# Feed-forward blocks taken in pairs with one down phase, the layer-2 start without norm edges, and a wider bonus product, in a two-layer RWKV-7 / S5 trunk

## The chip, the cores and the metric

The kernel runs on one core of a Trainium2 chip. The metric is the device time in microseconds of one execution, from the first to the last instruction. The engines named below are PE (TensorE, matrix products), PEld (its load of the stationary operand), DVE (VectorE), ACT (ScalarE), POOL (GpSimd) and SP (SyncE, which issues most DMAs).

## The reference

A sequence of 1024 frames of 1024 features passes two layers. Layer 0 mixes the frames by RWKV-7 (16 heads of 64), layer 1 by a diagonal complex state-space layer (S5) with a gated output; each mixer is followed by a squared-ReLU feed-forward part of width 4096, and every sub-layer ends in a layer norm of `alpha * h + f(h)`.

```python
def sq_relu_mlp(x, w1, w2):
    return jnp.square(jax.nn.relu(x @ w1)) @ w2
...
    bonus = jnp.sum(rh * kh * r_k.astype(f32), axis=-1, keepdims=True) * vh
    o = o + bonus.reshape(bsz, seq, d)
    return (o.astype(x.dtype) * g) @ wo
...
    for i in range(DEPTH):
        ...
        h = layer_norm(DN_ALPHA * h + mix, ln_g[2 * i], ln_b[2 * i])
        h = layer_norm(DN_ALPHA * h + sq_relu_mlp(h, mlp_w1[i], mlp_w2[i]),
                       ln_g[2 * i + 1], ln_b[2 * i + 1])
```

## The kernel before

**Tiles.** Features lie on the 128 partitions, frames on the free axis. The 1024 frames are two halves of 512 columns, A (tiles `hA`, operands `oAh`/`oAl`) and B (`hB`, `oBh`/`oBl`); a half of the residual is 8 tiles of 128x512.

**Dense products.** Each operand is split into a rounded high part and the rest. `mm3` (L258, through `mmb`, so that most rows have L256) computes one 128x128 by 128x512 product as three matmuls: high weight by high data, high weight by low data, low weight by high data. A weight comes by DMA into `wraw` (SP), ACT casts it to `whi` (L191), DVE takes the rest into `wlo` (L192); four buffers of each.

**Feed-forward part.** The width of 4096 is 16 blocks of 256 (`KB2` = 2 tiles). `up(b)` computes two 128x512 tiles, 24 matmuls each, and turns each into a pair of operands: ACT takes relu (L1126) and square (L1127) and casts the high part into `qbuf` (L191), DVE takes the low part (L192). This is called the power chain here. `down(b)` runs over the 8 output tiles: each gets 6 matmuls (2 tiles by 3) into a PSUM tile `d`, and DVE adds that to the residual tile `hA` or `hB` (L1158; L1156, which also scales, for the first block). `mlp` runs up(0), then for each block up(b+1), down(b), and yields once a block, so that between an up and its own down phase lie the 48 matmuls of the next up.

**Bonus.** In `elem` of the RWKV part, each of 16 calls computes the bonus sums of two heads in eight chunks of 64 frames: 16 products of a 64x64 piece of `kf` by a column of `rksel` into `pb` (L648), then one DVE copy to `bo` (L650).

**Order.** The program is written step by step, but a scheduler with a timeline model orders every engine's queue by the rank of each step and by its estimate of when the operands are there. A few edges are fixed by hand: `weave` puts steps of a second generator (a norm, splits of weights) behind chosen DVE adds, `inorder` and `behind` fix neighbours. INS1 and INS3 say after how many turns of a feed-forward part the next part's code is emitted; PACEU, PACED and PREB set how much is woven in.

**PSUM.** The products `d` of the RWKV and layer-1 feed-forward parts take turns in three banks. One bank, tag "l", is shared by the triangular inverse of the RWKV units (`pv`, and the lines from L716 on, 30 steps on DVE one after the other, L716 and L718) and by the layer norm's sums (`pm` L989, `pq` L934, `pr` L957). Two banks are for "a" and two for "c". From the layer-2 feed-forward part on, `d` has seven.

**Stages in time** (us from the start of the profiled execution): loads and the RWKV projections to 120; the RWKV units of both halves with the projections and the output product `wo` (its adds are L1110) to about 770, in which the norm of A (LN1: means `pm`, centring L993, variance `pq`, L939 to L942 the result and its split) stands at 681 to 714; feed-forward of A with `wo` of B; from 1010 the S5 tables beside it; S5 of A (1300 to 1410); feed-forward of B with S5 of B at 1665 to 1790; the gates; from 1904 layer 2's feed-forward part, where three blocks (`JB`) of A are done alone with the norm of B woven into the adds of `da(0)` and `da(1)`, thirteen blocks are done for both halves together by `both`, and three of B at the end. The last two of these run in column halves of 256, with the last norm (`last_norm`, L1036 to L1088) of the first half under the products of the second.

Of the kernel before, what the change touches and what calls it, by code (L numbers as in the profile page):

```python
# [18 lines left out]
HT = 512  # L19
KT = 8  # L20
L = 64
KB2 = 2
INS1 = 12
INS2 = 13
VSH = (-1, 2, 2, 4, 64)
INS3 = 12
# [6 lines left out]
TB = 2  # L33
# [3 lines left out]
PACEU = (2.0, 7.0)  # L37
PACED = (0.5, 1.3)
PREB = 3
JB = 3  # L40
# [39 lines left out]
def trunk(ctx, tc, A):  # L80
# [123 lines left out]
    nw = [0]  # L204
# [373 lines left out]
    def elem(m):  # L578
# [5 lines left out]
        for j in range(2):  # L584
# [60 lines left out]
            for c in range(8):  # L645
                for h in range(2):
                    hs, bs = slice(64 * h, 64 * h + 64), slice(64 * (1 - h), 64 * (1 - h) + 64)
                    PE.matmul(pb[bs, c : c + 1], kf[hs, c * L : (c + 1) * L], rksel[hs, n0 + c // 4, h : h + 1],  # L648
                              start=True, stop=True)
            V.tensor_copy(ci(D.bo), pb[:, 0:8].rearrange("p (i c) -> p i c", i=2))  # L650
# [463 lines left out]
    def blocks(i, h, xo, qbuf):  # L1114
# [27 lines left out]
        def down(b, first=False, cs=slice(0, HT), keep=None):  # L1142
            for n2 in range(C // nw):
                if keep is None:
                    w = wload(A["mw2"][i, b, n2], KB2, nw, ("mw2", i, b, n2))
                else:
                    if (b, n2) not in keep:
                        keep[b, n2] = kept(A["mw2"][i, b, n2], low[("mw2", i, b, n2), 0])
                    w = keep[b, n2]
                for n in range(nw // 128):  # L1150
                    p = psd()[:, cs]
                    dense(p, [(x[:, n * 128 : (n + 1) * 128], y[:, n * 128 : (n + 1) * 128]) for x, y in w],
                          [(x[:, cs], y[:, cs]) for x, y in qs[b]])
                    z = h[n2 * (nw // 128) + n][:, cs]
# [7 lines left out]
    def mlp(i, h, xo, qbuf):  # L1162

        nb = 32 // KB2
        up, down = blocks(i, h, xo, qbuf)
        up(0)
        for b in range(nb):
            if b + 1 < nb:
                up(b + 1)
            down(b, b == 0)  # L1170
            yield
# [484 lines left out]
    first_steps(second_half(), 99000)  # L1656
    for b in range(JB - 1):
        ua(b + 1)
        da(b, b == 0)
    unweave()  # L1660
# [11 lines left out]
    da(JB - 1, JB == 1)  # L1672
# [12 lines left out]
    for b in range(JB - TB):  # L1685
        ub(b + 1)
        db(b)
    for b in range(JB - TB + 1, JB):
        ub(b)
    keep = {}  # L1690
    for c in range(2):
        for b in range(JB - TB, JB):
            db(b, False, slice(256 * c, 256 * c + 256), keep)
# [78 lines left out]
```

## Time and profile before

| | |
|---|---|
| median of 3 runs | 2558.89 us (2570.18, 2558.74, 2558.89) |
| profiled execution | 2565.43 us |
| its span | 2563.6 us |
| mean granted TensorE clock | 0.973 of full speed |
| PE busy | 2470.6 us in 16684 records |
| DVE busy | 1784.2 us in 3443 |
| ACT busy | 1213.8 us in 2165 |
| POOL busy | 409.6 us in 336 |
| DMA | 340.66 MB, mean 133 GB/s |

Busy time is the time in which an engine has an instruction under way. PE is busy 96% of the span, but its matmuls overlap, and a busy PE is not yet PE at its peak; what remains to be gained or lost by a new order is in the stretches where it stands still, 93 us in all, and in the stretches where the granted clock is under 1. So the profile is read stage by stage, by the idle time of PE in each, and then by what ended that idle time.

### The profile page before, as it was taken

The numbers are of one execution on the slowest core, as the hardware profiler recorded it, in microseconds if no ns is written. First come the engines' busy times: TensorE is split into PE (matmuls) and PEld (weight loads), VectorE is DVE, ScalarE is ACT, GpSimd is POOL, SyncE is SP. The second block draws the span as 40 slices with busy tenths as digits, with TensorE's granted clock in tenths as the row PEclk, the third lists the DMA queues.
The fourth block names the chain that finished last, engine by engine and source line by source line (L and its number), as shares of the span: only waits on it lengthen the run. The fifth ranks groups of instructions, "written<-read, shape, count | busy, mean of one in ns | idle before, by whom it ended". The sixth has DMA issues, their size and how long they took to land.

```text
span 2563.6 us, 43894 instructions
## 1 busy us (share of the span) xinstructions
PE 2470.6 (96%) x16684; PEld 2012.9 (79%) x16684; DVE 1784.2 (70%) x3443; ACT 1213.8 (47%) x2165; POOL 409.6 (16%) x336
## 2 busy tenths in 40 slices
PE   7999999999889999999998999999999999999997
PEld 5778777788768877877787788887887888888887
DVE  7478686687696867989876665676748555555556
ACT  7556665555354444345543444343555333333434
POOL 3111333232212011001000000100223111111101
PEclk9999998989899999999999999999999999999999
DMA  5875555654222335246556553244351111111233
GB/s 167 279 229 194 185 169 164 215 176 134 77 63 85 97 92 168 92 120 174 151 198 238 173 180 108 95 158 164 103 190 62 46 54 54 50 54 47 82 116 115
DMA packets 217682, 340.66 MB, mean 133 GB/s; under 512 B 21248, under 2 KB 81792, under 8 KB 217472
## 3 DMA queue, kind: packets, MB, share of 16 engines
q1 hardware_dynamic: 216320, 335.77, 41.3%
q8 instruction: 131, 2.15, 0.4%
q10 hardware_dynamic: 1152, 2.10, 0.2%
q14 instruction: 79, 0.65, 0.1%
HBM read 267.53 MB, written 70.25 MB: 132 GB/s over the span
## 4 chain that ended last, share of the span: by engine, by line
PE 79%; DVE 10%; DMA 5%; ACT 4%; issue 2%; POOL 0%; SPq 0%; ACTq 0%; DVEq 0%; POOLq 0%
PE d L256 59%; PE d L1195 9%; PE pA L672 1%; PE pR L780 1%; DVE wlo L192 1%; DVE oAl L192 1%; PE pX L785 1%; PE pk L1427 1%; DVE xh L718 1%; DVE x L716 1%; PE pU L790 1%; PE pq L934 1%; PE pb L648 1%; PE pO L801 1%; PE pO L799 1%
## 5 line engine op out<-in xcount | busy, mean ns | idle before, releaser
L191 ACT CAST whi<-wraw 128x512 fp32r<-128x512 f32 x424 | 262.2, 620 | 431.9 <-PE d L256 351.3
L192 DVE TENSOR_TENSOR wlo<-wraw,whi 128x512 fp32r<-128x512 f32 x424 | 308.6, 730 | 198.6 <-ACT whi L191 187.4
L256 PE MATMUL d<-qbuf,whi 128*128 128x512 f32 x1152 | 366.4, 399 | 9.5 <-ACT rl L1126 5.7
L256 PE MATMUL d<-oAh,whi 128*128 128x512 f32 (+1 forms) x752 | 303.5, 409 | 10.5 <-ACT ev L493 4.9
L256 PE MATMUL d<-oAl,whi 128*128 128x512 f32 (+1 forms) x752 | 300.8, 402 | 6.5 <-DVE oAl L942 4.4
L256 PE MATMUL d<-oAh,wlo 128*128 128x512 f32 (+1 forms) x752 | 301.7, 403 | 0.0
L256 PEld LDWEIGHTS d<-qbuf,whi 128*128 128x128 f32 x1152 | 213.7, 190 | 60.4 <-ACT rl L1126 7.4
L256 PE MATMUL d<-qbuf,wlo 128*128 128x512 f32 x576 | 227.7, 396 | 0.0
L256 PE MATMUL d<-oBh,whi 128*128 128x512 f32 x496 | 196.5, 397 | 0.0
L256 PE MATMUL d<-oBh,wlo 128*128 128x512 f32 x496 | 195.1, 394 | 0.0
L256 PE MATMUL d<-oBl,whi 128*128 128x512 f32 x496 | 194.8, 393 | 0.0
L256 PEld LDWEIGHTS d<-oAh,whi 128*128 128x128 f32 (+1 forms) x752 | 143.5, 192 | 45.3 <-ACT ev L493 6.3
L256 PEld LDWEIGHTS d<-oAl,whi 128*128 128x128 f32 (+1 forms) x752 | 143.7, 192 | 37.5 <-DVE oAl L942 4.8
L256 PEld LDWEIGHTS d<-oAh,wlo 128*128 128x128 f32 (+1 forms) x752 | 143.8, 192 | 30.9 <-issue 1.0
L256 PE MATMUL d<-qh,wlo 128*128 128x512 f32 x416 | 163.1, 392 | 0.0
L256 PE MATMUL d<-qh,whi 128*128 128x512 f32 x416 | 162.5, 394 | 0.0
L256 PE MATMUL d<-ql,whi 128*128 128x512 f32 x416 | 161.9, 389 | 0.0
L256 PEld LDWEIGHTS d<-qbuf,wlo 128*128 128x128 f32 x576 | 109.2, 190 | 23.5
L1158 DVE TENSOR_TENSOR hB<-hB,d 128x512 f32<-128x512 f32 (+1 forms) x160 | 98.0, 630 | 26.3 <-PE d L256 25.3
L256 PEld LDWEIGHTS d<-oBh,wlo 128*128 128x128 f32 x496 | 93.4, 188 | 21.2 <-issue 0.6
L1158 DVE TENSOR_TENSOR hA<-hA,d 128x512 f32<-128x512 f32 x136 | 91.9, 681 | 26.1 <-PE d L256 25.1
L256 PEld LDWEIGHTS d<-oBh,whi 128*128 128x128 f32 x496 | 93.6, 189 | 20.8 <-issue 0.9
(495 smaller groups left out, 5292.3 us busy)
## 6 DMA issues: line engine op xcount, KB each, us to landing
wraw<-in_mw_dram SPq DMA_DIRECT2D x356, 256.0 KB, 2.8
wlo<-low SPq DMA_DIRECT2D x92, 256.0 KB, 3.0
wraw<-in_glu_dram SPq DMA_DIRECT2D x64, 256.0 KB, 2.7
low<-wlo SPq DMA_DIRECT2D x52, 256.0 KB, 3.3
raw<-in_mw_dram SPq DMA_DIRECT2D x52, 256.0 KB, 2.6
wraw<-in_wk_dram SPq DMA_DIRECT2D x32, 256.0 KB, 3.5
wraw<-in_wr_dram SPq DMA_DIRECT2D x32, 256.0 KB, 4.4
wraw<-in_wv_dram SPq DMA_DIRECT2D x32, 256.0 KB, 4.9
```

Of the source, the lines that this page charges most:

```text
L191: S.copy(hi, src)
L192: op = (e or V).tensor_sub(lo, src, hi.bitcast(F32))
L256: bulk.append((PE.matmul(p, w, x, **kw).ins, x.shape[-1]))
L648: PE.matmul(pb[bs, c : c + 1], kf[hs, c * L : (c + 1) * L], rksel[hs, n0 + c // 4, h : h + 1], start=True, stop=True)
L672: prods.append(PE.matmul(pp[h][:, cc, i], D.KB[j][hs, u].rearrange("p j l -> p (j l)"), D.AR[j][hs, u].rearrange("p j l -> p (j l)"), star ...
L716: V.tensor_mul(tv, xa[:, s + 1 : 32, s : s + 1].broadcast_to([128, nt, w]), xv[:, s : s + 1, 0:w].broadcast_to([128, nt, w]))
L718: V.tensor_add(xv[:, s + 1 : 32, 0:w], xv[:, s + 1 : 32, 0:w], tv)
L780: hop.append(PE.matmul(pR[hs, i], at[:, h, c, i, 0], vsa[:, cl, h, i], start=True, stop=True))
L785: hop.append(PE.matmul(pX[hs, i], xt[hs, NP * c + i], R[hs, i], start=True, stop=True))
L790: hop.append(PE.matmul(pU[hs, i], D.kbt[i // 2, c // 2][:, c % 2, i % 2, hs], vsa[:, cl, h, i], start=True, stop=True))
L1158: weave(V.tensor_add(z, z, p), PACED[i])
L1195: PE.matmul(p, w[:, k], x, start=not add and k + j == 0, stop=k == 3 and j == 2, skip_group_check=True)
```

## The change

There are four edits.

1. `down` takes a tuple of blocks. Its two PSUM tiles for a pair of output tiles are summed over all blocks of the tuple, so that DVE adds once an output tile instead of once a block and output tile. For the first pair of output tiles the last block's two parts come last, one by one. `mlp` runs up(b), up(b+1), down((b, b+1)): 8 turns instead of 16, with INS1 and INS3 at 6 instead of 12, and other paces.
2. At the start of layer 2 the norm of B is emitted in one piece under rank 99000, without the edges of `weave`, ahead of up(1); da((0, 1)) follows, then up(2), the sums for `both`, and da((2,)).
3. In the last stage the first of B's three blocks has its down phase after up(1), and the last two share one down phase in each column half.
4. The bonus sums of both heads and two chunks of 64 frames come from one product of 128x128 by 2 columns: 4 products a call instead of 16. Four small copies (two on DVE, two on ACT) take the place of one.

```diff
-INS1 = 12
+INS1 = 6
...
-INS3 = 12
+INS3 = 6
...
-PACEU = (2.0, 7.0)
-PACED = (0.5, 1.3)
-PREB = 3
+PACEU = (2.0, 6.0)
+PACED = (0.5, 2.0)
+PREB = 1
...
-            for c in range(8):
-                for h in range(2):
-                    hs, bs = slice(64 * h, 64 * h + 64), slice(64 * (1 - h), 64 * (1 - h) + 64)
-                    PE.matmul(pb[bs, c : c + 1], kf[hs, c * L : (c + 1) * L], rksel[hs, n0 + c // 4, h : h + 1],
-                              start=True, stop=True)
-            V.tensor_copy(ci(D.bo), pb[:, 0:8].rearrange("p (i c) -> p i c", i=2))
+            for tt in range(4):
+                PE.matmul(pb[:, 2 * tt : 2 * tt + 2], kf[:, tt * 128 : (tt + 1) * 128], rksel[:, n0 + tt // 2],
+                          start=True, stop=True)
+            pbv = pb[:, 0:8].rearrange("p (i c h) -> p c i h", i=2, c=2)
+            for h in range(2):
+                for e in range(2):
+                    (V.tensor_copy if e == 1 - h else S.copy)(
+                        D.bo[64 * (1 - h) : 64 * (1 - h) + 64, e::2, 2 * j : 2 * j + 2],
+                        pbv[64 * e : 64 * e + 64, :, :, h])
...
-        def down(b, first=False, cs=slice(0, HT), keep=None):
+        def down(bs, first=False, cs=slice(0, HT), keep=None):
             for n2 in range(C // nw):
...
-                for n in range(nw // 128):
-                    p = psd()[:, cs]
-                    dense(p, [(x[:, n * 128 : (n + 1) * 128], y[:, n * 128 : (n + 1) * 128]) for x, y in w],
-                          [(x[:, cs], y[:, cs]) for x, y in qs[b]])
-                    z = h[n2 * (nw // 128) + n][:, cs]
+                nn = nw // 128
+                ps = [psd()[:, cs] for _ in range(nn)]
+                parts = [(w[k], qs[b][k]) for w, b in zip(ws, bs) for k in range(KB2)]
+
+                def products(n, js):
+                    for j in js:
+                        (x, y), (qh, ql) = parts[j]
+                        sl = slice(n * 128, (n + 1) * 128)
+                        mm3(ps[n], x[:, sl], y[:, sl], qh[:, cs], ql[:, cs], j == 0, j == len(parts) - 1)
+
+                last = len(parts) - 1
+                groups = [range(KB2 * m, KB2 * m + KB2) for m in range(len(bs))]
+                if n2 == 0 and len(bs) > 1:
+                    groups[-1:] = [(j,) for j in groups[-1]]
+                turns_ = [(n, js) for js in groups for n in range(nn)]
+                for n, js in turns_:
+                    products(n, js)
+                    if last not in js:
+                        continue
+                    z, p = h[n2 * nn + n][:, cs], ps[n]
...
-        up(0)
-        for b in range(nb):
-            if b + 1 < nb:
-                up(b + 1)
-            down(b, b == 0)
+        for b in range(0, 32 // KB2, 2):
+            up(b)
+            up(b + 1)
+            down((b, b + 1), b == 0)
             yield
...
     ua(0)
-    first_steps(second_half(), 99000)
-    for b in range(JB - 1):
-        ua(b + 1)
-        da(b, b == 0)
-    unweave()
+    with rank(99000):
+        run(second_half())
+    ua(1)
+    da((0, 1), True)
+    ua(2)
...
-    da(JB - 1, JB == 1)
+    da((2,))
...
-    for b in range(JB - TB):
-        ub(b + 1)
-        db(b)
-    for b in range(JB - TB + 1, JB):
-        ub(b)
+    ub(1)
+    db((0,))
+    ub(2)
     keep = {}
     for c in range(2):
-        for b in range(JB - TB, JB):
-            db(b, False, slice(256 * c, 256 * c + 256), keep)
+        db(tuple(range(JB - TB, JB)), False, slice(256 * c, 256 * c + 256), keep)
```

**What stands where.** The edits also move instructions that they do not touch, since the scheduler orders everything anew. Three places show it; after the change most lines have a number that is 3 higher up to about L1140 and about 20 higher behind it.

The first is PE where the output product of half A (`d<-oA`, weights `whi` and `wlo`) runs out and LN1's mean `pm<-hA` comes. Before, `pm<-hA` follows a few rows behind the last dense product:

```order
L256 MATMUL d<-oAh,wlo 128x512
L256 MATMUL d<-oAh,whi 128x512
L648 MATMUL pb<-rksel,kf 64x1 x3
L672 MATMUL pA<-AR,KB 128x128
L648 MATMUL pb<-rksel,kf 64x1 x13
L256 MATMUL d<-oAl,whi 128x512
L256 MATMUL d<-oAh,wlo 128x512
L790 MATMUL pU<-vsa,kbt 64x64 x8
L799 MATMUL pO<-st,AR 64x64 x8
L801 MATMUL pO<-vsa,AT_7131 64x64 x8
L672 MATMUL pA<-AR,KB 128x128 x2
L989 MATMUL pm<-hA,ones_c 128x512
```

After, the same engine goes from the last dense product into a run of small products of the RWKV units:

```order
L256 MATMUL d<-oAl,whi 128x512
L256 MATMUL d<-oAh,wlo 128x512
L793 MATMUL pU<-vsa,kbt 64x64 x8
L802 MATMUL pO<-st,AR 64x64 x8
L804 MATMUL pO<-vsa,AT 64x64 x8
L611 MATMUL pss<-hsel,sq 128x2 x4
L783 MATMUL pR<-vsa,AT 64x64 x8
L788 MATMUL pX<-o,XT 64x64 x8
L619 MATMUL pn<-ident,sq 128x128 x4
```

and comes to the mean 24 rows behind that last dense product, at the end of this piece:

```order
L740 MATMUL pv_7294<-XT,x_7220 32x32 x32
L619 MATMUL pn<-ident,sq 128x128 x4
L646 MATMUL pb<-rksel,kf 128x2 x4
L788 MATMUL pX<-o,XT 64x64
L992 MATMUL pm<-sa,ones_c 128x512
L992 MATMUL pm<-sb,ones_c 128x512
L992 MATMUL pm<-hA,ones_c 128x512
```

So the dense products of `wo` no longer lie among the last unit's small products.

The second place is DVE there: the adds of `wo` (L1110 before, L1113 after) against the steps of the fifth unit's inverse (`x` and `xh`, L716 and L718 before, L719 and L721 after). Before, six of the eight adds come behind the inverse's step of 128x117; the last of them stands 7 rows ahead of LN1's centring (L993):

```order
L650 COPY bo<-pb 128x2x4
L1110 SCALAR_TENSOR_TENSOR hA<-hA,d 128x512
L844 SCALAR_TENSOR_TENSOR o<-o,vr,lg 128x64
L793 TENSOR_TENSOR st<-pU,st 128x256
L844 SCALAR_TENSOR_TENSOR o<-o,vr,lg 128x64 x7
L192 TENSOR_TENSOR wlo<-wraw,whi 128x512
L794 TENSOR_TENSOR st<-st,PL 128x256
L622 SCALAR_TENSOR_TENSOR ldsg<-cmask,ldsg 128x512
L993 TENSOR_TENSOR hA<-hA,pm 128x512 x8
```

After, the eighth add stands right ahead of that step, 67 rows ahead of the centring (L996), and one split of a weight (L192) follows it:

```order
L847 SCALAR_TENSOR_TENSOR o<-o,vr,lg 128x64 x6
L789 COPY vsa<-pX 64x256
L721 TENSOR_TENSOR xh<-xh,x_7220 128x14x9
L1113 SCALAR_TENSOR_TENSOR hA<-hA,d 128x512
L719 TENSOR_TENSOR x_7220<-xa,xh 128x117
L192 TENSOR_TENSOR wlo<-wraw,whi 128x512
L721 TENSOR_TENSOR xh<-xh,x_7220 128x13x9
L796 TENSOR_TENSOR st<-pU,st 128x256
L719 TENSOR_TENSOR x_7220<-xa,xh 128x120
```

So the inverse and the following unit's element work now lie wholly between the last add and the norm.

The third place is PE in a feed-forward part of layer 1, half B, at the start of a down phase (numbers tell the buffers apart; `d_16877` and `d_16878` are the first pair of output tiles, `d_16917` the next; `whi_16867` belongs to the pair's first block, `whi_16873` and `whi_16913` to blocks of the second). After the change it reads, from the last product of the up phase:

```order
L256 MATMUL d_16823<-oBh_12255,wlo_16833 128x512
L256 MATMUL d_16877<-qbuf_9489,whi_16867 128x512 x2
L256 MATMUL d_16877<-qbuf_9489,wlo_16868 128x512
L256 MATMUL d_16877<-qbuf_9489,whi_16867 128x512 x2
L256 MATMUL d_16877<-qbuf_9489,wlo_16868 128x512
L256 MATMUL d_16878<-qbuf_9489,whi_16867 128x512 x2
L256 MATMUL d_16878<-qbuf_9489,wlo_16868 128x512
```

and the products that use the second tile of the up phase just ended come here, first by the high part of `q` (single rows), then by the low and the high:

```order
L256 MATMUL d_16917<-qbuf_9489,whi_16913 128x512 x2
L256 MATMUL d_16917<-qbuf_9489,wlo_16914 128x512
L256 MATMUL d_16877<-qbuf_9489,whi_16873 128x512
L256 MATMUL d_16878<-qbuf_9489,whi_16873 128x512
L256 MATMUL d_16917<-qbuf_9489,whi_16913 128x512
L256 MATMUL d_16877<-qbuf_9489,whi_16873 128x512
L256 MATMUL d_16877<-qbuf_9489,wlo_16874 128x512
```

Between the two pieces' first and last rows stand 27 matmuls before the first use of that tile's high part and 30 before the first use of its low part; before the change it was the 48 matmuls of the following up phase.

More of the change, by code (lines that the diff above doesn't have):

```diff
@@ L1140, in kept @@
             return [(hi[:, k], lo[:, k]) for k in range(KB2)]
-        def down(b, first=False, cs=slice(0, HT), keep=None):
+        def down(bs, first=False, cs=slice(0, HT), keep=None):
             for n2 in range(C // nw):
[L1144 to L1149, printed above, removed]
-                for n in range(nw // 128):
-                    p = psd()[:, cs]
-                    dense(p, [(x[:, n * 128 : (n + 1) * 128], y[:, n * 128 : (n + 1) * 128]) for x, y in w],
-                          [(x[:, cs], y[:, cs]) for x, y in qs[b]])
-                    z = h[n2 * (nw // 128) + n][:, cs]
+                ws = []
+                for b in bs:
+                    if keep is None:
+                        ws.append(wload(A["mw2"][i, b, n2], KB2, nw, ("mw2", i, b, n2)))
+                    else:
+                        if (b, n2) not in keep:
+                            keep[b, n2] = kept(A["mw2"][i, b, n2], low[("mw2", i, b, n2), 0])
+                        ws.append(keep[b, n2])
+                nn = nw // 128
[16 more added lines that the diff above has]
+                    z, p = h[n2 * nn + n][:, cs], ps[n]
                     if first:
@@ L1162, in mlp @@
     def mlp(i, h, xo, qbuf):
-        nb = 32 // KB2
         up, down = blocks(i, h, xo, qbuf)
-        up(0)
-        for b in range(nb):
-            if b + 1 < nb:
-                up(b + 1)
-            down(b, b == 0)
+        for b in range(0, 32 // KB2, 2):
+            up(b)
+            up(b + 1)
+            down((b, b + 1), b == 0)
             yield
```

## The prediction

> **What bounds the kernel now.** First the page: busy time by engine, and the slices of PE and of its granted clock.
>
> ```profile
> PE 2470.6 (96%) x16684; PEld 2012.9 (79%) x16684; DVE 1784.2 (70%) x3443; ACT 1213.8 (47%) x2165; POOL 409.6 (16%) x336
> PE   7999999999889999999998999999999999999997
> PEclk9999998989899999999999999999999999999999
> ```
>
> PE is the bound nearly everywhere: of 2563.6 us it stands still for 93. In the chain of waits one stretch of products shows their pace:
>
> ```profile
> 1416.88 103.08 PE d L256 x449
> ```
>
> 103.08 / 449 = 0.2296 us a matmul of 512 columns, without a gap. The change leaves the number of these matmuls as it is, so only idle time, small products and clock can move. The table of stages (start:end, length, busy of PE, PEld, DVE, ACT, POOL with counts, clock, DMA share, GB/s) says where the idle time is:
>
> ```profile
> 0.00:120.00 120.00, 102.64 (x442) 77.47 (x443) 72.69 (x129) 76.51 (x134) 30.88 (x36) 0.96 0.65 218
> 120.00:655.00 535.00, 511.99 (x5018) 423.41 (x5017) 406.27 (x963) 308.79 (x579) 146.97 (x127) 0.94 0.57 183
> 655.00:712.00 57.00, 45.06 (x419) 37.66 (x417) 33.56 (x60) 24.04 (x44) 15.09 (x11) 0.79 0.20 62
> 712.00:770.00 58.00, 51.28 (x430) 40.76 (x431) 53.52 (x143) 32.04 (x60) 13.29 (x11) 0.91 0.22 69
> 1010.00:1300.00 290.00, 285.68 (x1493) 227.37 (x1495) 254.85 (x482) 145.95 (x261) 22.43 (x15) 0.99 0.50 141
> 1300.00:1410.00 110.00, 103.45 (x1193) 84.55 (x1188) 81.52 (x176) 42.83 (x77) 0.00 (x0) 0.98 0.65 226
> 1665.00:1790.00 125.00, 121.78 (x1312) 99.89 (x1311) 88.03 (x167) 47.67 (x86) 1.29 (x1) 0.97 0.49 163
> 1904.00:1960.00 56.00, 53.05 (x230) 41.44 (x230) 46.61 (x68) 34.81 (x62) 25.19 (x17) 1.00 0.30 98
> 1960.00:2430.00 470.00, 470.00 (x2052) 385.72 (x2051) 268.39 (x402) 174.88 (x295) 76.34 (x57) 1.00 0.18 57
> 2518.00:2563.60 45.60, 31.59 (x243) 29.86 (x242) 31.50 (x88) 18.52 (x39) 6.16 (x9) 0.87 0.26 93
> ```
>
> Length minus PE busy: 17.4 and 23.0 us in the first two, 11.9 around LN1 (clock 0.79), 6.7 behind it; 4.3 beside the S5 tables, 6.6 and 3.2 in the two S5 parts, 3.0 at layer 2's start, none for 470 us, 14.0 at the end. Most of what can move lies in the RWKV part, which the change touches only by the bonus and by moved instructions.
>
> **Part 1: fewer adds.** The groups of the adds, and of the products that follow them:
>
> ```profile
> L1158 DVE TENSOR_TENSOR hB<-hB,d 128x512 f32<-128x512 f32 (+1 forms) x160 | 98.0, 630 | 26.3 <-PE d L256 25.3
> L1158 DVE TENSOR_TENSOR hA<-hA,d 128x512 f32<-128x512 f32 x136 | 91.9, 681 | 26.1 <-PE d L256 25.1
> L256 PE MATMUL d<-qbuf,whi 128*128 128x512 f32 x1152 | 366.4, 399 | 9.5 <-ACT rl L1126 5.7 <-DVE hA L1158 2.2 <-DVE hA L1156 1.5
> ```
>
> With the 24 adds of L1156 there are 320; the new order holds 168, so 152 go. At (98.0 + 91.9) / 296 = 0.64 us that is 97.5 us of DVE, a large number off the path: PE waited for these adds 2.2 + 1.5 = 3.7 us. What it waited for more, 5.7 us, is relu freeing a bank. Most of this idle time lies in the tables' and S5 stages, where DVE is busy 254.85 of 290 us beside PE; in the new order the S5 part of A is spread over pairs 6 and 7 of 8, and should idle like that of B, 3.2 us instead of 6.6. I put the relief at **-5 us** (0 to -10, since 4.3 + 6.6 = 10.9 us is all there is in both stages).
>
> **Part 2: the down phase comes sooner.** A calm power chain, from the first product of a down phase on:
>
> ```profile
> 1498.08 0.63 PE L256 MATMUL d<-qbuf,whi 128*128 128x512 f32 x2
> 1498.58 0.59 ACT L1126 ACTIVATE rl<-d 128x512 f32<-128x512 f32 x1
> 1499.87 0.62 ACT L191 CAST qbuf<-rl 128x512 fp32r<-128x512 f32 x1
> 1500.52 0.69 DVE L192 TENSOR_TENSOR qbuf<-rl,qbuf 128x512 fp32r<-128x512 f32 x1 [0.16 <-ACT qbuf L191]
> ```
>
> Relu starts 0.5 us behind the up phase's end, and the low part is there at 1501.21, 3.1 us behind it. Before, 48 matmuls (11.0 us) covered it; now 27 lie ahead of the high part's first use, 6.2 us, and 30 ahead of the low part's, 6.9. Calm stages pay nothing. Beside the tables a chain of before looks like this:
>
> ```profile
> 1149.81 0.59 ACT L1126 ACTIVATE rl<-d 128x512 f32<-128x512 f32 x1
> 1155.91 0.60 ACT L191 CAST qbuf<-rl 128x512 fp32r<-128x512 f32 x1
> 1157.79 1.77 DVE L192 TENSOR_TENSOR qbuf<-rl,qbuf 128x512 fp32r<-128x512 f32 x1
> ```
>
> 1159.56 - 1149.81 = 9.75 us, and 0.5 ahead of it: beyond 6.9 by 3.4. A block is 96 matmuls, 22 us; 290 us hold six pairs, so the bounds are 0 and 6 x 3.4 = 20 us. Since this was the longest of the stage, and the relieved DVE and the scheduler's order work against it, I take a value near the lower end, **+2**.
>
> **Part 3: the bonus.** Three neighbours on PE's timeline:
>
> ```profile
> 660.06 1.10 PE L648 MATMUL pb<-rksel,kf 64*64 64x1 f32 x32
> 661.08 1.05 PE L611 MATMUL pss<-hsel,sq 128*128 128x2 f32 x8
> 662.00 0.31 PE L686 MATMUL pT<-ident,KB 128*128 128x128 f32 x1
> ```
>
> A call of before takes 661.08 - 660.06 = 1.02 us up to the next start. The new call has the shape of `pss`: 662.00 - 661.08 = 0.92. Sixteen calls: 16 x 0.10 = **-1.6 us** (0 to -4). The four small copies are not on a path: `bo` is first used in the group norm, a unit later.
>
> The Trainium skill ("TensorE: Matmul & The Clock Gate", section "LDWEIGHTS (loading the stationary operand)") has a load take its number of columns over 1.2 ns, whatever its rows: an estimate by it is 32 x 53 ns = 1.7 us a call before and 8 x 107 ns = 0.85 after, 13.6 us over 16 calls, which would bring the sum to -12.4. The trace speaks against that here, since 32 loads and products took 1.02 us together.
>
> **Part 4: LN1's hole, the largest term.** The order shows that all dense products of half A's `wo` now run out before the inverse of unit 5 reaches its 128x117 step, while LN1's mean still has to wait for the bank "l" that this inverse holds. The stretch of before from that step to LN1's centring (window of the stages' table), and in it three groups of DVE and one of PE:
>
> ```profile
> 629.70:681.50 51.80, 49.50 (x529) 38.58 (x528) 43.27 (x97) 23.94 (x45) 17.11 (x15) 0.97 0.33 103
> L192 DVE TENSOR_TENSOR wlo<-wraw,whi 128x512 fp32r<-128x512 f32 x11 | 7.9, 722 | 3.0 <-ACT whi L191 3.0
> L1110 DVE SCALAR_TENSOR_TENSOR hA<-hA,d 128x512 f32<-128x512 f32 x6 | 4.1, 679 | 0.3 <-PE d L256 0.3
> L980 DVE TENSOR_TENSOR sb<-sb,hA 128x512 f32<-128x512 f32 x2 | 1.4, 690 | 0.0
> L256 PE MATMUL d<-oAl,whi 128*128 128x512 f32 x39 | 15.8, 404 | 0.0
> ```
>
> PE has 39 x 3 = 117 dense matmuls there, 117 x 0.2296 = 26.9 us of its 49.5; 22.6 us are small products. In the new order the dense ones have gone ahead, and some 2 us of the rest (`pA`) stand behind the mean: 20.7 remain. Of DVE's 43.27 us, ten of the eleven L192 (7.2), the adds (4.1) and sums for the mean (2.1) go ahead: 29.9 remain, one after the other. DVE also waited 51.80 - 43.27 = 8.5 us; 3.0 + 0.3 of it go with the moved instructions, up to 5.2 (on small products and ACT) may stay. The stretch is then 29.9 to 35.1 us with 20.7 of PE work: 9.2 to 14.4 us idle, where before had 51.8 - 49.5 = 2.3. I take the middle, **+9.5 us**. The ends are wider, as the norm's own variance shows:
>
> ```profile
> 686.57 13.79 PE L934 MATMUL pq<-ones_c,sq 128*128 128x1 f32 x64 [5.23 <-DVE hA L993]
> 2507.98 0.95 PE L1013 MATMUL pq<-ones_c,sq 128*128 128x1 f32 x8
> ```
>
> 64 records took 13.79 us at a clock of 0.60 in that window, 215 ns each; in the second row it is 119. At full clock the norm would be 6 us shorter, so -6 is one end (the hole filled, and the clock up); the other is a hole of the full 35 us with PE's 20.7 us slowed to half as well, +20.
>
> Elsewhere in the RWKV units the dense products are spread anew: six groups of chains have more of them in front (I take -3), another run of small products ahead of the feed-forward part has fewer (+2). Together **-1** (-6 to +6, a quarter of the 23.0 us idle of 120 to 655 either way).
>
> **Part 5: the start of layer 2.** Without edges the norm of B ends some 150 products ahead of `both` in the new order, before 84: **-2.5** of the 3.0 us idle in 1904 to 1960 (0 to -3).
>
> **Part 6: the end.** Before, DVE finishes adds and a variance behind the last product:
>
> ```profile
> 2541.54 0.76 DVE L1158 TENSOR_TENSOR hB<-hB,d 128x256 f32<-128x256 f32 x2
> 2543.20 0.43 DVE L1055 TENSOR_TENSOR sq<-sq 128x256 f32<-128x256 f32 x1
> 2544.78 0.16 DVE L1068 TENSOR_SCALAR rs<-pq 128x2 f32<-128x2 f32 x1 [1.15 <-PE pq L1065]
> 2546.61 1.03 PE L1045 MATMUL pm<-sab,ones_c 128*128 128x256 f32 x4
> ```
>
> In the new order `rs` stands ahead of the last add, so the 1.15 us wait and part of the adds go: **-1.8** (0 to -3.5).
>
> **The sum.** -5 + 2 - 1.6 + 9.5 - 1 - 2.5 - 1.8 = -0.4 us. The profiled execution took 2565.43 and would take 2565.0; it lies 6.5 above the median of 2558.89, near which two of three runs lie, so on the scale of the median I forecast **2558.5 us**: no difference. A measurement of this kernel tells about 0.5% (12.8 us) from no change.
>
> **The rivals.**
> - *The hole stays shut, and the tables gain all they can.* The RWKV term is 0 instead of 9.5, the relief -10 instead of -5: 2558.5 - 14.5 = 2544. For it speaks that ACT and DVE are the slower engines there; against it the order, which has no dense product left to put there. Chance 0.18.
> - *The down phase waits for its own up.* In the pairs beside tables and S5, ACT and DVE are too late with the power chain, as in the 9.75 us row; the price is 20 instead of 2: 2576.5, slower than before. It decides from a chain of over 6.9 us behind the up phase on. For it speak that row and a DVE at 254.85 of 290; against it that the scheduler knows the new distance, and that 97 us of adds go. Chance 0.20.
> - *The bonus pays by columns.* If the columns loaded set a call's time, 32 loads of 64 (2048) become 8 of 128 (1024), and half of the 1.02 us goes: -8.2 over 16 calls instead of -1.6, so 2551.9. Against it stand the 0.92 us of `pss`, which loads 1024 already. Chance 0.03. (This is the rule of the Trainium skill named above, section "LDWEIGHTS (loading the stationary operand)".)
> - *The change does less than it says:* the adds go, but nothing waited for them, and nothing else moves: 2558.9 less 1.6 for the bonus, 2557.3. This falls within the forecast.
>
> **How the numbers follow.** Forecast with its small variants 0.58, first rival 0.18, second 0.20, third 0.03, other slower mishaps 0.01. The range reaches from the first rival to the second, 2544 to 2577. Faster by over 0.5% (under 2546.1): the first rival, 0.18; slower (over 2571.7): the second and the mishaps, 0.21; within: the forecast and the third, 0.61.
>
> **What would show it.** Right: PE's row of LN1's `pq` stays near 13.8 us, the stretch ahead of it idles about 12 us, the idle of 1010 to 1410 falls by some 5, no wait of `d<-qbuf` on L191 or L192 over a microsecond. Wrong: waits on `qbuf` of 3 us a pair, a clock under 0.9 outside the RWKV part, or a `pb` call under 0.3 us.

## The result, and the profile after

| | before | after |
|---|---|---|
| median of 14 runs each | 2570.22 us | 2552.82 us |
| ratio after / before, 95% interval | | 0.9947 (0.9937 to 0.9958) |
| profiled execution | 2565.43 us | 2551.81 us |
| its span | 2563.6 us | 2550.0 us |
| PE busy | 2470.6 us | 2464.4 us |
| DVE busy | 1784.2 us | 1713.5 us |

The change makes the kernel 0.53% faster (0.42 to 0.63), some 13.6 us, where the forecast was 0.4: just beyond the 0.5% up to which it was to count as no difference, with an interval that takes in that 0.5%. The two medians alone lie 17.4 us apart (0.68%); the ratio is used below. One of the 14 runs of before took 12113.2 us, for which the record gives no reason. The measured 2552.82 lies within the forecast range. The 14 runs of before have their median 11 us above that of the first three, so the differences below are ratios to before within one group of runs, and 0.1% is 2.6 us.

The page of the kernel after, in the rows shown of before: busy time by engine, the slices of PE and its clock.

```profile
PE 2464.4 (97%) x16300; PEld 2008.4 (79%) x16300; DVE 1713.5 (67%) x3307; ACT 1217.8 (48%) x2197; POOL 413.2 (16%) x336
PE   7999999999899999999999999999999999999998
PEclk9999989999789999999999999999999999999999
```

The two profiled executions differ by 13.6 us as well: 6.2 us of PE's busy time, and 7.4 of its idle time (93.0 against 85.6). Only the idle time is steady: the changed kernel profiled once more (e5 below) stands still for 85.2 us, but is busy for 2474.2, so executions of one kernel differ in busy time by more than those 6.2 us. Windows cut at the same events say where. LN1's variance starts at 686.57 before and 686.71 after, and 770 lies behind the last RWKV unit in both. Columns: start:end, length, busy of PE, PEld, DVE, ACT, POOL, clock, DMA share, GB/s. First before, then after:

```profile
0.00:686.60 686.60, 638.86 (x5743) 519.08 (x5743) 502.95 (x1134) 400.22 (x740) 191.92 (x172) 0.94 0.58 186
686.60:770.00 83.40, 72.11 (x562) 60.23 (x563) 63.09 (x159) 41.15 (x75) 14.30 (x12) 0.83 0.16 48
770.00:1660.00 890.00, 876.24 (x5634) 706.77 (x5634) 665.40 (x1256) 399.72 (x706) 63.29 (x48) 1.00 0.46 141
1660.00:2480.00 820.00, 813.84 (x4336) 665.83 (x4335) 499.65 (x775) 333.02 (x570) 129.03 (x93) 1.00 0.28 89
```

```profile
0.00:686.60 686.60, 631.12 (x5356) 514.88 (x5356) 506.71 (x1139) 404.20 (x765) 187.93 (x171) 0.94 0.58 185
686.60:770.00 83.40, 79.52 (x602) 66.43 (x603) 62.55 (x156) 43.04 (x82) 14.53 (x11) 0.80 0.17 50
770.00:1660.00 890.00, 882.52 (x5631) 709.76 (x5630) 601.43 (x1151) 402.97 (x716) 71.05 (x50) 1.00 0.46 142
1660.00:2480.00 820.00, 813.94 (x4352) 666.22 (x4351) 499.32 (x768) 331.64 (x568) 128.73 (x92) 1.00 0.29 91
```

PE's idle time (length less busy) goes from 47.7 to 55.5 ahead of LN1's variance, from 11.3 to 3.9 behind it, from 13.8 to 7.5 in the layer-1 feed-forward parts with the tables and S5 of A, and stays at 6.2 and 6.1 to 2480. Not all of the 7.8 us ahead of LN1's variance is the hole. The stretch of the prediction's Part 4, from the inverse's step of 128x117 to LN1's centring (629.7 to 681.5 before), is this one after:

```profile
646.30:681.70 35.40, 29.24 (x366) 23.19 (x362) 29.65 (x75) 18.69 (x39) 14.27 (x14) 0.71 0.22 69
```

It idles 6.2 us where before had 2.3, so the hole is +3.9. The 5 us from the centring to the variance are the same in both, and the other 4.0 lie ahead of that step (44.4 us idle against 40.4). The stretch right behind the variance gives back 7.4, and the clear gain is the 6.3 us from 770 to 1660, where DVE is busy 64 us less.

**The hole and what follows it.** PE's timeline after, with the wait ahead of a row in brackets:

```profile
644.81 0.39 PE L256 MATMUL d<-oAh,wlo 128*128 128x512 f32 x1
...
652.21 1.11 PE L619 MATMUL pn<-ident,sq 128*128 128x128 f32 x4 [1.55 <-ACT sq L616]
...
678.44 1.20 PE L992 MATMUL pm<-hA,ones_c 128*128 128x512 f32 x2
...
686.71 13.78 PE L937 MATMUL pq<-ones_c,sq 128*128 128x1 f32 x64 [5.37 <-DVE hA L996]
700.42 1.12 PE L793 MATMUL pU<-vsa,kbt 128*64 128x64 f32 x16
...
711.58 0.79 PE L256 MATMUL d<-oAl,whi 128*128 128x512 f32 x1 [0.62 <-DVE oAl L945]
...
750.41 1.11 PE L793 MATMUL pU<-vsa,kbt 128*64 128x64 f32 x16 [1.52 <-ACT vsa L790]
```

The last dense product stands at 644.81, the mean's last part at 678.44, and nothing but small products and the mean's first parts lies between. Before, the rows that answer to the last two had these waits, and the small products that now start at 700.42 stood behind the first of them:

```profile
711.90 0.79 PE L256 MATMUL d<-oAl,whi 128*128 128x512 f32 x1 [4.36 <-DVE oAl L942]
...
714.76 0.83 PE L790 MATMUL pU<-vsa,kbt 128*64 128x64 f32 x16
...
749.45 1.12 PE L790 MATMUL pU<-vsa,kbt 128*64 128x64 f32 x16 [4.36 <-ACT vsa L787]
```

Both shrink (4.36 to 0.62, 4.36 to 1.52). For the first the rows show how: `oAl` is hardly sooner there (the product that waits for it starts 25.3 us behind the variance's start before, 24.9 after), but `pU` and the two groups of `pO` that follow it now run ahead of it, from 700.42 to 703.57, and fill the wait. For the second, `pU` starts 2.2 us behind the `pX` ahead of it instead of 5.0; what made that step shorter was not looked into. The groups of the adds, and of the products behind them, after:

```profile
L256 PE MATMUL d<-qbuf,whi 128*128 128x512 f32 x1152 | 364.6, 397 | 5.5 <-ACT qbuf L191 4.1 <-DVE hA L1178 1.3
...
L1178 DVE TENSOR_TENSOR hB<-hB,d 128x512 f32<-128x512 f32 (+1 forms) x80 | 49.1, 629 | 23.6 <-PE d L256 23.4
...
L1178 DVE TENSOR_TENSOR hA<-hA,d 128x512 f32<-128x512 f32 x64 | 42.4, 681 | 23.7 <-PE d L256 23.5
```

Waits of 5.7 on relu and 3.7 on adds have become 1.3 on adds, and 4.1 on the power chain, which is the new price of the shorter way from up to down: 0.85 of it in layer 1, at 1121 us, and 3.29 at the start of layer 2 (Part 5 below).

**The bonus.** The group of its products, before and after:

```profile
L648 PE MATMUL pb<-rksel,kf 64*64 64x1 f32 x512 | 20.3, 202 | 0.8 <-POOL kf L643 0.8
```

```profile
L646 PE MATMUL pb<-rksel,kf 128*128 128x2 f32 x128 | 20.3, 278 | 3.4 <-POOL kf L643 3.4
```

A quarter of the records in the same 20.3 us. But six of the sixteen calls after the change fell in stretches of lower clock, two of them in the hole, and took 1.44 to 1.73 us each. At a granted clock of 1.00 in both, one call before and one after read:

```profile
763.70 1.10 PE L648 MATMUL pb<-rksel,kf 64*64 64x1 f32 x32
764.72 1.05 PE L611 MATMUL pss<-hsel,sq 128*128 128x2 f32 x8
```

```profile
765.22 0.95 PE L646 MATMUL pb<-rksel,kf 128*128 128x2 f32 x8
766.03 1.03 PE L611 MATMUL pss<-hsel,sq 128*128 128x2 f32 x8
```

From start to next start that is 1.02 us before and 0.81 after.

### The profile page after: what moved, and what is told of

Its sections match the earlier page's. It is cut to its first block, busy times and chain, and to the rows that moved or that the text cites. A ratio compares the mean times of both kernels' runs of the same rounds, so it can differ in the third digit from the quotient of the medians.

```text
span 2550.0 us, 42959 instructions
## 1 busy us (share of the span) xinstructions
PE 2464.4 (97%) x16300; PEld 2008.4 (79%) x16300; DVE 1713.5 (67%) x3307; ACT 1217.8 (48%) x2197; POOL 413.2 (16%) x336
## 4 chain that ended last, share of the span: by engine, by line
PE 55%; DVE 2%; ACT 1%; DMA 1%; POOL 0%; issue 0%; ACTq 0%; DVEq 0%
PE d L256 41%; PE d L1213 10%; PE pk L1445 1%; PE pu L1484 1%; PE pbu L1496 1%; PE py L1556 1%; PE py L1548 0%; PE pu L1477 0%; PE pyt L1566 0%; DVE oBl L192 0%; POOL sq L1008 0%; PE pb L1461 0%; DMA tb<-tB 0%; DVE t1r L1683 0%; PE pq L1016 0%
## 5 line engine op out<-in xcount | busy, mean ns | idle before, releaser
L191 ACT CAST whi<-wraw 128x512 fp32r<-128x512 f32 x424 | 261.9, 620 | 440.6 <-PE d L256 348.2
L192 DVE TENSOR_TENSOR wlo<-wraw,whi 128x512 fp32r<-128x512 f32 x424 | 311.9, 738 | 224.0 <-ACT whi L191 216.5
L256 PEld LDWEIGHTS d<-oBl,whi 128*128 128x128 f32 x496 | 93.1, 188 | 21.4 <-issue 0.7
L1272 DVE TENSOR_TENSOR hA<-hA,d 128x512 f32<-128x512 f32 x104 | 71.3, 686 | 47.2 <-PE d L256 47.2
```

Source lines behind the costliest of these rows:

```text
L191: S.copy(hi, src)
L192: op = (e or V).tensor_sub(lo, src, hi.bitcast(F32))
L256: bulk.append((PE.matmul(p, w, x, **kw).ins, x.shape[-1]))
L1272: V.tensor_add(z, z, p)
```

## The experiments

Each kernel was timed against the kernel before in its own group of runs.

| run | ratio to before | 95% interval |
|---|---|---|
| e1_no_bonus: edits 1 to 3 | 0.9956 | 0.9942 to 0.9970 |
| e2_bonus_only: edit 4 | 1.0019 | 1.0003 to 1.0035 |
| e3_old_start: without edit 2 | 0.9960 | 0.9945 to 0.9976 |
| e4_old_tail: without edit 3 | 0.9973 | 0.9962 to 0.9985 |
| e5_change_again: the change | 0.9942 | 0.9920 to 0.9964 |
| e6_add_per_block | 1.0045 | 1.0031 to 1.0060 |
| e7_norm_bank | 0.9932 | 0.9911 to 0.9953 |
| e8_norm_bank_old_bonus | 0.9966 | 0.9952 to 0.9980 |
| e9_dve_load | 1.0016 | 1.0004 to 1.0029 |
| e10_pairs_only: edit 1 | 0.9968 | 0.9957 to 0.9980 |
| e11_norm_bank_c | 0.9962 | 0.9948 to 0.9977 |
| e12_dve_load_both | 0.9953 | 0.9936 to 0.9970 |

### Which edit carries it: e1, e2, e10, e3, e4

**e1_no_bonus**, the diff against the changed kernel:

```diff
-            for tt in range(4):
-                PE.matmul(pb[:, 2 * tt : 2 * tt + 2], kf[:, tt * 128 : (tt + 1) * 128], rksel[:, n0 + tt // 2],
...
+            for c in range(8):
+                for h in range(2):
...
+            V.tensor_copy(ci(D.bo), pb[:, 0:8].rearrange("p (i c) -> p i c", i=2))
```

> Edits 1 to 3 with the old bonus (16 products of 64x64 and one copy a call). The order of the RWKV units is then that of before, with six adds of wo beside the fifth unit's inverse. Theory 1 (the edits add up: the pairs act behind 770 us, the bonus edit acts ahead of it): 7 to 9 us faster than before, ratio 0.9965 to 0.9973. Rival (the pairs also fill the waits that stood at 707 to 760 us, right behind LN1, and the bonus gives nothing): 11 to 14 us faster, 0.9946 to 0.9957.

**e2_bonus_only** is the reverse: the same lines of the change in the kernel before.

> Edit 4 alone: the new bonus product in the kernel of before. The order of the RWKV units is that of the changed kernel, with the hole ahead of LN1. The prediction's terms: 8 us slower (hole +9.5, bonus -1.6), ratio 1.003. Theory 1 (the hole costs 7.6 us of idle time, but the 2138 dense products ahead of LN1 run 6.7 us faster because the granted clock falls less often): 0 to 6 us faster, 0.9977 to 1.000. Rival: no difference beyond 2 us either way, 0.9992 to 1.0008.

Measured: 0.9956 without the bonus, 1.0019 with the bonus alone. The pairs and what goes with them carry the gain; the bonus edit alone is slower by 0.3 to 3.5 parts in a thousand (5 us), and beside the pairs its effect can't be told from nothing (0.9947 and 0.9942 against 0.9956). e1 lies at the edge of the rival's band, but not by the rival's way: in e1 the wait at 707 us is 4.36 as before, so the pairs did not fill it. In e2 the same windows, cut where LN1's variance starts in that execution, show the order at work without the pairs:

```profile
0.00:693.10 693.10, 634.99 (x5356) 517.55 (x5357) 508.10 (x1139) 403.26 (x765) 188.29 (x171) 0.93 0.57 184
693.10:777.00 83.90, 78.16 (x581) 64.91 (x582) 63.06 (x151) 42.35 (x80) 16.33 (x12) 0.76 0.16 46
```

58.1 us idle ahead of it (before 47.7) and 5.7 behind (before 11.3): the hole and the repayment both come from the order that the bonus edit brings about. They are not what it costs, though: from that inverse's step (652.8) to 777 PE idles 17.2 us in e2, and from the same step (629.7) to 770 it idles 18.7 in before. What this trace idles more lies ahead of the step (46.6 against 40.4) and from 770 to 1660. It is also the slowest of the run's twelve executions (2583.0, median 2572.45), and their granted clock is lower than that of before (0.969 against 0.974 in the mean), so what makes up the 5 us is open. The prediction's sum for the edit, 8 us slower, lies in the interval (0.8 to 9), the middle of which is 5; theory 1's 0 to 6 us faster falls, and the rival of no difference but for its last tenths.

**e10_pairs_only** puts the old start and the old last stage (the diffs of e3 and e4) into e1.

> Edit 1 alone: pairs in both layer-1 feed-forward parts, with the old bonus, the old start of layer 2 and the old last stage. If the edits add up, this is the run without the bonus (0.9956) less what the start (some 3 us) and the last stage (2 to 7 us) give: 0.9970 to 0.9990. Theory 1 as first written (the start gives nothing, the last stage 1.8 us): 0.9960 to 0.9966.

Measured 0.9968 (0.9957 to 0.9980): 8 us from edit 1 alone, between the two bands, with an interval that takes in part of either. Edits 2 and 3 together then make 3 us (0.9968 to e1's 0.9956), not the 10 to which e3 and e4 add up.

**e3_old_start**, against the changed kernel:

```diff
-    with rank(99000):
-        run(second_half())
-    ua(1)
-    da((0, 1), True)
-    ua(2)
+    first_steps(second_half(), 99000)
+    for b in range(JB - 1):
+        ua(b + 1)
+        da((b,), b == 0)
+    unweave()
```

> The changed kernel with the start of layer 2 as it was: the norm of B woven into the adds, blocks 0 to 2 of A one by one. The prediction's term (-2.5 for the edit): 2.5 us slower than the changed kernel, ratio to before 0.9957. Theory 1 (the idle time there is 3.43 us after against 2.95 before, so nothing was gained): within 1 us of the changed kernel, 0.9943 to 0.9951.

**e4_old_tail**, against the changed kernel:

```diff
-    ub(1)
-    db((0,))
-    ub(2)
+    for b in range(JB - TB):
+        ub(b + 1)
+        db((b,))
+    for b in range(JB - TB + 1, JB):
+        ub(b)
...
-        db(tuple(range(JB - TB, JB)), False, slice(256 * c, 256 * c + 256), keep)
+        for b in range(JB - TB, JB):
+            db((b,), False, slice(256 * c, 256 * c + 256), keep)
```

> The changed kernel with the old last stage: blocks of B with a down phase of their own in each column half. The prediction's term (-1.8) and the profile after (45.65 us from the last norm of A to the end against 47.51) agree: 1.8 us slower than the changed kernel, ratio to before 0.9954. Rival: the last stage gives nothing, 0.9947.

Measured: 0.9960 and 0.9973, against 0.9947 and 0.9942 for the change. For the start the intervals overlap with either expectation: nothing is settled by the time. By the ratios the last stage is worth 7 to 8 us, more than the 1.8 us of the prediction, and e4's interval (0.9962 to 0.9985) leaves out both expectations. The traces do not show that size. From the start of the last product of `both` to the end, the four kernels with the old last stage (before, e2, e4, e10) took 80.5, 81.9, 82.6 and 81.9 us, and ten profiles with the new one 78.6 to 80.7, 80.2 in the mean: 1.5 us, near the forecast. What else slowed e4 stays open.

**e5_change_again** is the changed kernel itself.

> The changed kernel once more, as the measure for the other runs of this group. Ratio to before 0.9947 as recorded; 1 to 3 us faster than without the bonus edit if the bonus edit gives a little beside the pairs, 3 to 6 us slower if it costs what it cost alone.

Measured 0.9942 (0.9920 to 0.9964), the result on record once more. Against e1's 0.9956 the bonus edit gives at most a little beside the pairs.

### Whether the adds matter: e6, e9, e12

**e6_add_per_block** keeps the order of the pairs and gives each block its own down phase and add:

```diff
-            down((b, b + 1), b == 0)
+            down((b,), b == 0)
+            down((b + 1,))
```

> The changed kernel, but each pair of blocks ends in two down phases with an add for each block (up, up, down, down): the order of the pairs with the old number of adds in both layer-1 feed-forward parts (296 rows of adds of 512 columns and less, instead of 168). Theory 1 (PE waits for banks that the adds and relu hold, beside the S5 tables, and fewer adds shorten these waits): 5 to 7 us slower than the changed kernel, with waits on L1178, L1176 and relu of 6 us or more between 770 and 1660 us. Rival (the gain comes from the order up, up, down and the later S5 of A, not from the adds): within 2 us of it.

Measured 1.0045 (1.0031 to 1.0060): 26 us slower than the changed kernel in the same group (0.9942), four times what theory 1 expected. The rival falls. Group and window of this kernel:

```profile
L256 PE MATMUL d<-qbuf,whi 128*128 128x512 f32 x1152 | 368.4, 401 | 14.5 <-DVE hA L1178 5.1 <-DVE hB L1178 4.9 <-ACT qbuf L191 3.6
```

```profile
770.00:1660.00 890.00, 866.55 (x5553) 697.14 (x5553) 660.67 (x1262) 395.18 (x699) 58.70 (x45) 0.99 0.45 140
```

DVE is as busy as before (660.67 against 665.40), yet PE stands still 23.5 us there instead of 13.8: two down phases in a row call for sixteen adds in the time in which before eight adds were followed by 48 matmuls of an up phase. So the order of the pairs by itself costs, and the merged adds pay for it and for more. In this kernel S5 of A also came earlier again (its largest waits stand at 1366 to 1400 us, those of the change at 1550 to 1560), so part of the 26 us may be the scheduler's answer to the adds rather than the adds themselves.

**e9_dve_load** gives DVE the time back without the banks:

```diff
                         weave(V.tensor_add(z, z, p), PACED[i])
+                    if i == 0:
+                        V.tensor_tensor(z, z, z, op=ALU.max)
```

> The changed kernel with one more DVE instruction behind each add of the layer-1 feed-forward parts (128 in all): the residual tile's maximum with itself, 128x512, some 0.69 us each, which holds no PSUM bank and leaves the value as it is. DVE gets back the 88 us that the pairs took from it there, the banks are as in the changed kernel. Theory 1a (the gain of fewer adds is DVE time: DVE is the bound beside the tables and S5): 15 to 25 us slower than the changed kernel, ratio to before 1.000 to 1.004. Theory 1b (the gain is that a bank is held for fewer adds and that PE waits for fewer of them): within 4 us of the changed kernel, 0.9940 to 0.9958.

Measured 1.0016 (1.0004 to 1.0029), in the middle of theory 1a: about 18 us slower than the change, for 88 us of DVE instructions (DVE's busy time in the whole kernel rises by less, from 1713.5 to 1782.9). Theory 1b falls. The window:

```profile
770.00:1660.00 890.00, 875.48 (x5586) 700.44 (x5585) 665.45 (x1275) 398.43 (x707) 70.42 (x48) 1.00 0.45 141
```

DVE's busy time and PE's idle time (14.5 us) are back at what they were before. That is 7.0 us of the 18. The mean granted clock of the executions is lower as well (0.970 against 0.972 and 0.971 for the change), which may account for some more; where the rest lies was not settled. The added instructions stand right behind the adds, but did not act by delaying these, since the waits on adds in the window are 2.1 us against 1.3 in the change: the largest wait is 3.10 us on a weight's low part at 1142 us, others of 1.84 and 2.94 us are on the norm's and S5's operands. As in e6, the scheduler's answer to the new instructions is part of what was measured.

**e12_dve_load_both** puts such instructions where PE never waits:

```diff
                             V.tensor_add(z, z, p)
+                        if h is hQ:
+                            V.tensor_tensor(z, z, z, op=ALU.max)
```

> The changed kernel with 104 more DVE instructions of 128x512 in the down phases of layer 2's products for both halves (the residual tile of the second half, maximum with itself, some 0.69 us each, 72 us in all). There DVE is busy 267 of 470 us and PE never stands still. Theory 2 (a microsecond of DVE costs only where DVE is short, beside the RWKV units, the tables and S5): within 3 us of the changed kernel, 0.9940 to 0.9956. Rival (DVE time costs the same everywhere; 88 us cost some 18 us in the run with the load in layer 1, so 72 us cost 15): 0.9995 to 1.0010.

Measured 0.9953 (0.9936 to 0.9970): theory 2's band, outside the rival's. The stage's window in this kernel:

```profile
1960.00:2430.00 470.00, 470.00 (x2052) 385.07 (x2051) 321.54 (x491) 170.18 (x286) 77.54 (x54) 1.00 0.18 56
```

DVE has 321.54 us of work instead of 266.83 after the change, and PE still runs through. A microsecond of DVE cost 18 / 88 = 0.2 us in layer 1 and nothing that shows here, though the interval leaves room for 6 us in all.

### Whether the hole matters: e7, e8, e11

**e7_norm_bank**: LN1's sums in pool a.

```diff
-        pq = pl.tile([128, HT], F32, tag="l", name="pq")
+        pq = pa.tile([128, HT], F32, tag="a", name="pq")
...
-        pr = spread(pq)
+        pr = spread(pq, pa, "a")
...
-        pm = plt("pm")
+        pm = pa.tile([128, HT], F32, tag="a", name="pm") if by_pe else plt("pm")
```

> The changed kernel with LN1's sums (pm, pq, pr) in a bank of pool a instead of the bank that the inverse holds. LN1 then comes right behind wo, and the products of the next up phase are there while the inverse runs. Theory 1 (the hole is a real cost that the order behind it gives back only in part): 4 to 10 us faster than the changed kernel, idle time of PE from 640 to 770 us down from 15 to under 10 us. Rival (what the hole costs is given back behind it in full, so that closing it brings the waits behind LN1 back): within 2 us.

**e8_norm_bank_old_bonus** is the same with the old bonus.

> As the run before, with the old bonus. In its order dense products stand on both sides of LN1's sums and of the inverse. Theory 1 (the bonus edit only acts by the order that it brings about): 4 to 12 us faster than without the bonus edit and with the old bank, idle from 640 to 770 us under 10 us. Rival (the new bonus product is worth its own 1.6 us and more): slower than the kernel of the run before.

**e11_norm_bank_c** takes pool c instead of pool a.

> The changed kernel with LN1's sums in a bank of pool c instead of pool a. In its order the hole ahead of LN1 is cut to some 17 small rows, and the next up phase's products stand beside the rest of the inverse. If the hole costs its idle time less what the order behind gives back: 2 to 8 us faster than the changed kernel, 0.9912 to 0.9938. If it is given back in full: 0.9942 to 0.9948.

Measured: 0.9932, 0.9966 and 0.9962; the change is at 0.9942 and 0.9947, the pairs with the old bonus at 0.9956. None is clear of its neighbour: the intervals overlap, and e7's 2.6 us may be nothing. The theory that the hole costs fails in all three: e7 is short of 4 to 10 us, and e8 and e11 came out slower than the kernels that they alter, e11 outside both of its bands. That e8 is slower than e7 is what its rival said; the 9 us between them, with intervals that just touch, are far more than the 1.6 us of the bonus product, and nothing here explains them. The windows from 640 to 770 us show why so little comes of closing the hole, first for the kernel before, then the change, then e7:

```profile
640.00:770.00 130.00, 111.34 (x1020) 90.78 (x1019) 101.64 (x235) 62.02 (x113) 29.85 (x24) 0.87 0.22 70
```

```profile
640.00:770.00 130.00, 114.31 (x1008) 93.71 (x1007) 103.18 (x257) 66.04 (x129) 32.30 (x27) 0.79 0.20 61
```

```profile
640.00:770.00 130.00, 113.94 (x1026) 95.72 (x1025) 107.05 (x249) 66.74 (x131) 32.08 (x27) 0.79 0.21 64
```

PE idles 18.7, 15.7 and 16.1 us (17.7 in e8, 17.5 in e11, and from 15.5 to 18.7 in every run): LN1's variance starts at 652.50 in e7 instead of 686.71, and the idle time only moves. It comes back where the dense products have run ahead of the last unit's chain:

```profile
719.49 1.12 PE L793 MATMUL pU<-vsa,kbt 128*64 128x64 f32 x16 [4.94 <-ACT vsa L790]
...
727.80 1.75 PE L675 MATMUL pA<-AR,KB 64*128 64x128 f32 x16 [2.77 <-DVE AT L679]
```

By the idle time the rival holds for e7: what the hole costs is given back behind it. The ratio alone, with its interval, would not decide.

## Why the prediction was right in its range and wrong in its size

**Part 4, the hole, is the term that missed most: right as a mechanism and nearly in its length, too large as idle time, and wrong as a cost.** The stretch from the inverse's step to the centring was to be 29.9 to 35.1 us long and is 35.4. But 6.2 us of it are idle, not 9.2 to 14.4, so the hole is +3.9 and not +9.5: PE's small products, taken at the 20.7 us that they had at a granted clock of 0.97, took 29.2 at 0.71. The prediction's sign, about 12 us idle ahead of the variance, is met from 640 us on (11.9), but only with the 5 us behind the centring, which before had as well. The variance took 13.78 us, as said. Elsewhere ahead of the hole the idle time rose by 4.0, where -1 (-6 to +6) stood. What was missed altogether is the step behind it: the sum closed the account at LN1, although PE waits for the norm's and the last unit's chains 25 and 64 us later, and these waits shrink. With the 7.4 us given back there, 59.0 us idle up to 770 became 59.4, and the term is about 0 in the profile. By the runs, the bonus edit that brings the order about gave 2 to 4 us beside the pairs (0.9956 to 0.9947 and 0.9942), where Parts 3 and 4 had it 6.9 slower.

**Part 1, the adds, was sized too small.** In idle time it came out as said: 13.8 us became 7.5 from 770 to 1660, -6.3 where -5 stood. But by the runs edit 1 gave 8 us (e10), where Parts 1 and 2 had 3. "A large number off the path" put 97.5 us of DVE at 5 us, and bounded it by the 10.9 us of idle time that before had in two stages. In the new order e9 measured 18 us for 88 us of DVE and e6 26 us for the adds themselves. So the bound seems wrong in kind: it read the price of the adds from the order of before, where 48 matmuls of an up phase gave DVE the time to catch up, while in the new one they would come twice as dense without the merging. That reading is argued from e6 and e9; neither separates the adds from the scheduler's answer.

**Part 2, the shorter way from up to down, was right.** PE waits 0.85 us on the power chain's casts in layer 1 (forecast 2, bounds 0 and 20). The rival that made of it 20 us, slower than before, did not come; e6 shows that the pair order has a price of another kind, on the adds.

**Part 3, the bonus:** -1.6 forecast, 0 by the groups (20.3 us in both), since part of the new calls ran at a lower clock. At a clock of 1.00 a call took 0.21 us less, 3.4 us over sixteen. The rival by columns of the Trainium skill ("TensorE: Matmul & The Clock Gate", section "LDWEIGHTS (loading the stationary operand)") does not come out by the same rows: half the columns took 0.81 us and not half of 1.02.

**Part 5, layer 2's start:** -2.5 forecast. In the profile the seven small waits of 0.2 to 0.6 us are gone, but one has come in their place, the third block's down phase right behind its own up:

```profile
1912.86 2.29 PE L256 MATMUL d<-qbuf,whi 128*128 128x512 f32 x7 [3.29 <-ACT qbuf L191]
```

3.0 us of idle time before, 3.4 after: the term is 0 there. It is the wait that Part 2 looked for in layer 1, at a place where the pair has no second block. By the prediction's own sign, no wait on L191 over a microsecond, this row was a miss.

**Part 6, the last stage**, -1.8: the last product and the last mean stand closer, 1.9 us apart from start to start (before 4.2, from 2542.45 to 2546.61).

```profile
2531.07 0.36 PE L256 MATMUL d<-qbuf,kt 128*128 128x256 f32 x1
...
2532.96 1.12 PE L1048 MATMUL pm<-sab,ones_c 128*128 128x256 f32 x4
```

As a mechanism it is as forecast, and by the traces, 1.5 us, in size too; e4's 7 to 8 us by ratio are not explained by it.

**The sum.** Forecast -0.4, measured -13.6. By the runs edit 1 gave 8 us instead of 3, edits 2 and 3 gave 3 instead of 4.3, and the bonus edit beside them gave 2 to 4 instead of costing 6.9. The largest miss is the hole and what follows it, the next the adds; each of these differences is uncertain by some 4 us. Of the first rival, "the hole stays shut, and the tables gain all they can" at 2544, the outcome has the size by ratio, and not the way: the hole opened, and it cost nothing because it was paid back.

**The range was met in part by luck.** Forecast and range stand on the first three runs of before, 2558.89. From the median of all 14, 2570.22, the same terms would have given 2569.8 and a range of 2555 to 2588, which 2552.82 misses; by the ratio, 0.9947 x 2558.89 = 2545.3, the outcome lies 1 us inside the lower end.

## What to carry to other kernels

The worth of removing work from an engine off the path could here be read neither from the waits on that work nor from the idle time of the old order; putting the same amount of harmless work back into the new kernel, stage by stage, and timing it says more, with the reservation that the scheduler answers to that work too. The stretch around LN1, bound by a serial chain, kept its idle time when the filler products were moved: closing the hole ahead of the chain opened one behind it, so an account of such a stretch has to run to the end of the chain. Grouping two producing phases and two consuming phases doubles the density of the consumer's work, and in this kernel paid only with that work merged too.

## What the runs showed of the hardware beyond that

A wait of PE can cost more than its length, when matmuls behind it run at a lower pace for a while. In the kernel before, on PE's timeline:

```profile
1011.59 0.82 PE L256 MATMUL d<-qbuf,whi 128*128 128x512 f32 x2 [2.37 <-ACT rl L1126]
...
1012.63 1.05 PE L256 MATMUL d<-qbuf,whi 128*128 128x512 f32 x2
1013.49 0.63 PE L256 MATMUL d<-qbuf,wlo 128*128 128x512 f32 x1
1013.91 1.06 PE L256 MATMUL d<-qbuf,whi 128*128 128x512 f32 x2
```

A microsecond behind the wait of 2.37 us, three matmuls take 1013.91 - 1012.63 = 1.28 us from start to start, where 3 x 0.2296 = 0.69 was the pace; the granted clock from 1012.63 to 1015.19 was 0.50. Not every wait is followed by that: behind the 3.10 us in e9 the matmuls kept their pace.

Nor do the waits explain the pace of the whole. Added up from each start to the next, without the waits, the 9182 records of `d` in the trace took 2078.6 us before and 2069.1 after. But the changed kernel profiled again took 2073.2, and e6, with the most idle time of all profiles (106.7 us), 2072.8. So 4 of those 9.5 us are what executions of one kernel differ by, and that the rest follows from waits is not shown.

The granted clock differs between the kernels, and the forecast took account of it in the bounds of Part 4 alone. The means over all recorded executions are 0.974 for before, 0.974 for e10, 0.972 and 0.971 for the change, 0.970 for e4 and e9, 0.969 for e2 and 0.968 for e6. Among the executions of one kernel, a clock lower by 0.001 went with a time longer by 1.1 to 2.3 us (straight lines through each group of nine or more). As an estimate from these figures, the 0.005 between before and e2 are 6 to 12 us, more than the 5 us by which the bonus edit alone was slower. No run was made to change the clock by itself.
